# Where in SBUF the split weights of four SwiGLUs begin

## The chip, the cores and the metric

One core of one Trainium2 chip runs the whole program. The metric is the device time of one execution in microseconds, as the median of several. A smaller number is better. Input arrays lie in HBM in the layout that the kernel wants; the output is the full trunk's output for 512 tokens of 1024 channels.

## The reference

Two layers of a streaming encoder, each with a SwiGLU, a mixer and a second SwiGLU. Only what the change touches, the SwiGLUs, is shown in full; the mixer has two attentions, a pooling branch and a gated sum.

```python
D_MODEL, SEQ, DEPTH, D_FF = 1024, 512, 2, 2816

def swiglu(h, w_gate, w_up, w_down):
    return (jax.nn.silu(h @ w_gate) * (h @ w_up)) @ w_down

def reference(x, c, ...):
    c_act = jax.nn.silu(c)
    for l in range(DEPTH):
        mod = (c_act @ w_ada[l] + b_ada[l]).reshape(B, N_MOD, D_MODEL)
        h = modulate(rms_norm(x, norm_gain[l, 0]), mod[:, 0], mod[:, 1])
        x = x + 0.5 * mod[:, 2][:, None, :] * swiglu(h, ffn_w_gate[l, 0], ffn_w_up[l, 0], ffn_w_down[l, 0])
        h = modulate(rms_norm(x, norm_gain[l, 1]), mod[:, 3], mod[:, 4])
        x = x + mod[:, 5][:, None, :] * hybrid_mixer(h, w_in[l], ...)
        h = modulate(rms_norm(x, norm_gain[l, 2]), mod[:, 6], mod[:, 7])
        x = x + 0.5 * mod[:, 8][:, None, :] * swiglu(h, ffn_w_gate[l, 1], ffn_w_up[l, 1], ffn_w_down[l, 1])
    return x
```

All numbers are float32.

## The kernel before

**Numbers.** Every float32 operand of a large product is split into a high part `hi` (float32r) and a low part `lo` (the rest). A product then takes three matmuls, issued by `triple` (lines 119 to 121): hi times hi, lo times hi, hi times lo. A matmul loads 128x128 numbers as the stationary operand ("weights", engine row PEld) and streams 256 or 512 columns of the other operand past them (row PE). In the profile's names `acc<-b,whi`, the streamed operand stands first and the stationary one second.

**Weights.** A block of weights of 512 KB comes by DMA from the SP queue into a `raw` buffer; ScalarE copies it to float32r (`hi`), VectorE subtracts (`lo`). `wchunk` (line 250) does this for one block at a time, into a buffer of the pool's tag `whi` and one of `wlo`, of which there are three each. In the text below such a block is a *plain chunk*. The loads for the next SwiGLU or mixer, which are made early, go to `ptb` and `b` buffers instead (`spare`).

**A SwiGLU** (class `Ffn`, instances (layer, which) = (0,0), (0,1), (1,0), (1,1)) goes through the 22 blocks of 128 hidden channels in four parts of 6, 6, 4 and 6 (`PARTS`). Each part computes gate and up for its blocks and then adds its share of the down projection to x. A part's blocks are taken in three ways:

- as plain chunks, with all 512 tokens streamed at once (512 columns): some blocks of part 0, and the up half of its pairs;
- in pairs (`gate_up_pair`, line 609): two blocks are multiplied as a 2 by 2 block matrix with the tokens in two halves, in seven block products instead of eight. A pair takes 7 products of 4 x 3 matmuls, each of 256 columns. `pair_weights` (line 527) loads the two blocks, and makes sums and differences of them. Gate pairs (`which` 0) hold their weights in `ptb`, `v2` and `strip`; up pairs (`which` 1, in parts 1 to 3: 8 pairs in each SwiGLU) hold three of the four weight blocks in `whi` and `wlo`, which serve six of the seven products, and the fourth in `v2`;
- the down projection (`k_outer`, line 384) takes plain chunks of 256 x 512 weights, and streams 512 columns, in the very last half 256.

**Order.** The program is written out by Python; a tile framework puts the waits in. Each engine takes its instructions in the order written. DMA issues stand in the queue of the engine that issues them; the SP queue is strictly in order, so an issue that waits holds all that stand behind it. A buffer of a tag may be written again when its last reader is done. A small load takes part in the change: `forget` (line 954) loads 64 numbers a partition of `w_f` into the one buffer `wf`, once a layer, at the start of the mixer; and `send` in `attention` (line 1084) copies row sums into the one buffer `flat`, eight times a layer, from which a DMA of the POOL queue stores them.

**Places in SBUF.** The pool lays its buffers one behind the other. In the built program the `whi`, `wlo`, `b`, `xv` and `v2` buffers begin at multiples of 512 bytes, and `hhi` and `hlo` (the normed input, split) at multiples of 256. `raw`, `pta`, `ptb` and `strip` begin 32 bytes past a multiple of 64. Slices used by one matmul lie a multiple of 512 bytes further in, so that these remainders hold for every matmul operand named here.

Of the kernel before, what the change touches and what calls it, by code (L numbers as in the profile page):

```python
# [40 lines left out]
def encoder_kernel(tc, xT, c, w_ada, b_ada, gains, w_gate, w_up, w_down, w_qkv, w_f, w_ubg,  # L41
# [208 lines left out]
    def wchunk(src, shape, side=True, spare=None, lo_eng=None, home=None):  # L250
        if lo_eng is None:
            lo_share[1] += 1
            lo_eng = nc.gpsimd if lo_share[0] and lo_share[1] % lo_share[0] == 0 else nc.vector
        if quiet[0] > 0:
            quiet[0] -= 1
            if quiet[0] == 0:
                gate.clear()
        elif side and flow["on"] and mod_tag[0] == "v2":
            side_work()
        raw = st([P] + list(shape), F32, *(home or (("b", NB) if spare else ("raw", NRAW))))  # L260
        last["dma"] = nc.sync.dma_start(raw, src).ins
        if spare == "ptb":
            both = st([P, 2] + list(shape), F32R, "ptb", 2)
            hi, lo = both[:, 0], both[:, 1]
        elif spare == "b":
            hi = st([P] + list(shape), F32R, "b", NB)
            lo = st([P] + list(shape), F32R, "b", NB)
        else:
            hi = st([P] + list(shape), F32R, "whi", 3)
            lo = st([P] + list(shape), F32R, "wlo", 3)  # L270
        with behind("scalar"):
            nc.scalar.copy(hi, raw)  # L272
        with behind("vector"):
            last["lo"] = lo_eng.tensor_tensor(lo, raw, hi.bitcast(F32), op=ALU.subtract).ins  # L274
        return hi, lo
# [167 lines left out]
    PARTS = (6, 6, 4, 6)  # L443
    UP_FROM = 1
    SPIN = (4, 0, 7, 3)


    class Ffn:
# [78 lines left out]
        def pair_weights(self, n, which=0):  # L527

            shape = [P, 2, 4, P]
            d = []  # L530
            if which:
                d = [(st(shape, F32R, "whi", 3), st(shape, F32R, "wlo", 3)) for _ in range(3)]
                both = st(shape, F32R, "v2", 4)
                e = (both[:, 0], both[:, 1])
            else:
                for _ in range(2):
                    both = st([P, 2] + shape[1:], F32R, "ptb", 2)
                    d.append((both[:, 0], both[:, 1]))
                d.append((st(shape, F32R, "v2", 4), st(shape, F32R, "v2", 4)))
                e = (st([P, 4, P], F32R, "strip", 2), st([P, 4, P], F32R, "strip", 2))  # L540
            r = [st(shape, F32, *(("raw", NRAW) if which else ("b", NB))) for _ in range(2)]
            for i in range(2):
                last["dma"] = nc.sync.dma_start(r[i].rearrange("p a k c -> p (a k) c"),
                                                (w_gate, w_up)[which][self.l, self.s, n + i]).ins
            s3 = st([P, 4, P], F32, "ssum", 1)
            a11, a12, a21, a22 = r[0][:, 0], r[0][:, 1], r[1][:, 0], r[1][:, 1]
            g = nc.vector.tensor_tensor

            def sums():
                split_to(*d[0], r[0])  # L550
                g(s3, a11, a21, op=ALU.subtract)
                g(a21, a21, a22, op=ALU.add)

            def more():
                g(a11, a21, a11, op=ALU.subtract)
                g(a12, a12, a11, op=ALU.subtract)
                split_to(*d[2], r[0])

            steps = [sums, lambda: split_to(*d[1], r[1]), more, lambda: split_to(*e, s3)]
            w = lambda i, j: (d[i][0][:, j], d[i][1][:, j])  # L560
            tiles = {"a11": w(0, 0), "a12": w(0, 1), "s1": w(1, 0), "a22": w(1, 1), "s2": w(2, 0), "s4": w(2, 1), "s3": e}
            return tiles, steps
# [99 lines left out]
        def run(self, nxt):  # L662
            l, s, ms = self.l, self.s, self.ms
            mod_tag[0] = "v2"
            f0 = 0
            for part, nf in enumerate(PARTS):
                flow.update(on=True, behind="norm", **ADA_FFN(l, s, part))
                acts = []
                n = 0
                if part == 0 and self.norm is None:  # L670
                    acts = self.start()
                    acts += self.plain((3, 4, 5), None)
                    n = 6
                elif part == 0:
                    g0, u0, g1 = self.pre
                    pg, pu, pg1 = mmt(), mmt(), mmt()
                    for hs in range(2):
                        self.norm.back(hs, acc if hs else mmt)
                        cols = slice(hs * HALF, (hs + 1) * HALF)
                        if hs == 0:  # L680
                            later(FRONT1, lambda: self.norm.front(1, acc))
                            later(BACK1, lambda: self.norm.back(1, acc))
                        for k in range(KD):
                            self.unit(pg, g0, cols, (k,))
                            self.unit(pu, u0, cols, (k,))
                        self.unit(pg1, g1, cols)
                        if hs == 0:
                            u1 = self.gate_up(1, 1)
                    acts.append(self.act(0, pg, pu))
                    pu1 = mmt()  # L690
                    self.unit(pu1, u1)
                    acts.append(self.act(1, pg1, pu1))
                    acts += self.plain((2, 3), self.norm)
                    n = 4
                if part == 0 and n < nf:
                    self.ready, steps = self.next_pair(4, True)
                    for z in steps:
                        z()
                while n < nf:
                    acts += self.gate_up_pair(f0 + n, n + 2 < nf, part >= UP_FROM)  # L700
                    n += 2
                mod_need(l, 3 * ms + 2)
                last = part == len(PARTS) - 1
                for c0 in (0, T):
                    def src(c):
                        r0 = (f0 + 2 * c) * P
                        return w_down[l, s, r0:r0 + 2 * P, c0:c0 + T].rearrange("(k p) c -> p k c", p=P)

                    def ops(hi, lo, kt, j):
                        return (hi[:, j * P:(j + 1) * P], lo[:, j * P:(j + 1) * P],  # L710
                                acts[kt][:, 0, :], acts[kt][:, 1, :])

                    if last and c0 == 0 and nxt is not None:
                        nxt.prefetch("v2")
                        mod_tag[0] = "raw"
                    split = last and c0 > 0
                    hook, then = None, None
                    if split:
                        hook = nxt.prefetch_weights if nxt is not None else (lambda: None)
                    elif c0 > 0:  # L720
                        def then(n=f0 + nf):
                            self.ready, steps = self.next_pair(n, not last)
                            for i, z in enumerate(steps):
                                later(8 * i, z)
                    for j, hs, o in k_outer(src, nf // 2, ops, hook, acc if c0 == 0 else mmt, then):
                        d = c0 // P + j
                        residual_tail(d, hs, o, modc[:, l, 3 * ms + 2, d:d + 1], nxt if last else None)
                        if last and nxt is None:
                            cols = slice(0, T) if hs is None else slice(hs * HALF, (hs + 1) * HALF)
                            nc.sync.dma_start(out[:, d, cols], xd(d)[:, cols])  # L730
                f0 += nf
# [273 lines left out]
    def attention(qs, ks, vs, strip, ys, filler, budget, group):  # L1005
# [78 lines left out]
        def send(p):  # L1084
            rs = st([P, 2 * NT], F32, "rs", 1)
            nc.vector.reciprocal(rs, sums[p])
            tp = mmt()
            nc.tensor.transpose(tp[:2 * NT, :P], rs, ident)
            flat = st([2 * NT, P], F32, "flat", 1)
            nc.scalar.copy(flat, tp[:2 * NT, :P])  # L1090
            pe[0] += 0.5
            nc.gpsimd.dma_start(inv_dram[group, p], flat)
            later(LAG_R, lambda: spread(p), group)
# [119 lines left out]
    class Mixer:  # L1213
# [10 lines left out]
        def run(self, nxt):  # L1224
            l = self.l
            flow["on"] = False
            for b in range(4):
                nc.gpsimd.dma_start(x_dram[b], x_blocks[b].rearrange("p a t -> p (a t)"))
            g = qkgc[:, l, :]
# [163 lines left out]
```

## Time and profile before

| | |
|---|---|
| median of 3 runs | 2378.53 us (2377.65 to 2382.12) |
| the profiled execution | 2377.12 us |
| its span, first to last instruction | 2375.4 us |
| PE / PEld busy | 2356.8 us (99%) / 2092.4 us (88%) |
| DVE / ACT / POOL busy | 1781.4 (75%) / 1168.7 (49%) / 190.6 us (8%) |
| DMA engines | 41% busy on average, 137 GB/s |

The profiled execution is 1.7 us longer than its span, and 1.4 us shorter than the median. A matmul's row has its start, which is measured, and a length whose end is modelled; successive matmuls overlap, so that the pace is the distance from start to start and not the length. The four SwiGLUs lie at about 0 to 372, 814 to 1211, 1211 to 1548 and 1990 to 2375 us of the span, with a mixer between the first two and between the last two.

### The profile page before, as it was taken

To read this page: it belongs to the slowest core of one execution; us is meant where nothing else is said; L and a number is where in the kernel's file an instruction comes from. 1 tells how busy PE (TensorE), PEld (TensorE's weight loads), DVE (VectorE), ACT (ScalarE), POOL (GpSimd) and SP (SyncE) were. 2 spreads that over 40 slices of the span, in tenths; PEclk is the share of its full clock that TensorE was granted. 3 is DMA by queue.
4 is the path that set the end of the run, shared out by engine and by line. 5 is a ranking of instruction groups with operands and counts; after the bars stand their busy time and mean duration, and the time that the engine had idled before them with its cause. 6 is when DMAs were issued, how large, how long until landed. Compare 5 with 4: busy or idle time off the path is not lost. (4 is left out here: it accounts for less than half of the span.)

```text
span 2375.4 us, 36727 instructions
## 1 busy us (share of the span) xinstructions
PE 2356.8 (99%) x14172; PEld 2092.4 (88%) x14172; DVE 1781.4 (75%) x3213; ACT 1168.7 (49%) x2048; POOL 190.6 (8%) x309
## 2 busy tenths in 40 slices
PE   8999999999999999999999999999999999999999
PEld 6898998788888898999998999988888888989998
DVE  7888876787678477888678778776866774767784
ACT  5354455676532353544554444556765324544452
POOL 2000002122220000000100000120222101000000
PEclk9999999999999999999999999999999999999999
DMA  7634433333367425344325333423243763223232
GB/s 278 207 104 155 148 125 99 95 98 120 123 211 265 154 68 187 111 137 150 109 87 188 128 104 134 160 89 99 87 136 114 260 233 133 89 98 123 64 116 89
DMA packets 118484, 325.19 MB, mean 137 GB/s; under 512 B 12034, under 2 KB 14338, under 8 KB 118308
## 3 DMA queue, kind: packets, MB, share of 16 engines
q1 hardware_dynamic: 115106, 314.38, 39.5%
q0 software_dynamic: 3200, 8.46, 1.1%
q8 instruction: 111, 1.82, 0.3%
q14 instruction: 65, 0.53, 0.1%
q10 hardware_dynamic: 2, 0.00, 0.0%
HBM read 316.35 MB, written 6.44 MB: 136 GB/s over the span
## 5 line engine op out<-in xcount | busy, mean ns | idle before, releaser
L272 ACT CAST whi<-raw 128x1024 fp32r<-128x1024 f32 (+1 forms) x260 | 270.4, 1044 | 345.5 <-PE acc L120 196.2
L274 DVE TENSOR_TENSOR wlo<-raw,whi 128x1024 fp32r<-128x1024 f32 (+1 forms) x254 | 310.1, 1225 | 155.1 <-ACT whi L272 153.2
L120 PE MATMUL acc<-b,whi 128*128 128x512 f32 (+1 forms) x704 | 261.1, 371 | 2.0 <-DVE b L381 2.0
L119 PE MATMUL acc<-b,whi 128*128 128x512 f32 (+1 forms) x704 | 262.3, 373 | 0.0
L121 PE MATMUL acc<-b,wlo 128*128 128x512 f32 (+1 forms) x704 | 260.4, 370 | 1.2 <-DVE wlo L274 1.2
L121 PE MATMUL mm<-b,wlo 128*128 128x256 f32 (+1 forms) x768 | 244.8, 319 | 0.3 <-DVE wlo L274 0.3
L120 PE MATMUL mm<-b,whi 128*128 128x256 f32 (+1 forms) x768 | 244.5, 318 | 0.0
L119 PE MATMUL mm<-b,whi 128*128 128x256 f32 (+1 forms) x768 | 244.5, 318 | 0.0
L198 DVE CUSTOM_DVE_ANT_0 v<-v,b,badac 128x1024 f32<-128x1024 f32 x144 | 187.2, 1310 | 19.6 <-DMA v<-in_w_ada_dram 19.5
L120 PE MATMUL mm<-hlo,whi 128*128 128x256 f32 (+1 forms) x616 | 199.1, 323 | 0.0
L121 PE MATMUL mm<-hhi,wlo 128*128 128x256 f32 (+1 forms) x616 | 199.0, 323 | 0.0
L119 PE MATMUL mm<-hhi,whi 128*128 128x256 f32 (+1 forms) x616 | 198.7, 323 | 0.0
L120 PE MATMUL acc<-hlo,whi 128*128 128x512 f32 x480 | 188.1, 392 | 1.7 <-DVE hlo L788 1.6
L119 PE MATMUL acc<-hhi,whi 128*128 128x512 f32 x480 | 187.9, 396 | 1.1 <-ACT hhi L785 1.1
L121 PE MATMUL acc<-hhi,wlo 128*128 128x512 f32 x480 | 187.6, 391 | 0.0
L380 ACT CAST whi<-raw 128x1024 fp32r<-128x1024 f32 x96 | 100.8, 1050 | 136.0 <-PE mm L120 68.0
L121 PEld LDWEIGHTS mm<-b,wlo 128*128 128x128 f32 x768 | 146.3, 190 | 11.2 <-DVE wlo L274 1.2
L120 PEld LDWEIGHTS mm<-b,whi 128*128 128x128 f32 x768 | 146.3, 191 | 10.2
L119 PEld LDWEIGHTS mm<-b,whi 128*128 128x128 f32 x768 | 146.3, 191 | 10.1
L120 PEld LDWEIGHTS acc<-b,whi 128*128 128x128 f32 x704 | 132.7, 189 | 25.2 <-DVE b L381 3.8
L121 PEld LDWEIGHTS acc<-b,wlo 128*128 128x128 f32 x704 | 132.6, 188 | 24.2 <-DVE wlo L274 1.7
L119 PEld LDWEIGHTS acc<-b,whi 128*128 128x128 f32 x704 | 132.7, 189 | 21.6
(326 smaller groups left out, 6116.9 us busy)
## 6 DMA issues: line engine op xcount, KB each, us to landing
v<-in_w_ada_dram SPq DMA_DIRECT2D x144, 512.0 KB, 4.8
raw<-in_w_down_dram SPq DMA_DIRECT2D x88, 512.0 KB, 3.9
raw<-in_w_up_dram SPq DMA_DIRECT2D x82, 512.0 KB, 3.6
b<-in_w_gate_dram SPq DMA_DIRECT2D x76, 512.0 KB, 6.0
raw<-in_w_ubg_dram SPq DMA_DIRECT2D x56, 512.0 KB, 4.1
raw<-in_w_qkv_dram SPq DMA_DIRECT2D x42, 512.0 KB, 4.0
raw<-in_w_branch_dram SPq DMA_DIRECT2D x24, 512.0 KB, 3.6
raw<-in_w_out_dram SPq DMA_DIRECT2D x16, 512.0 KB, 3.7
```

The lines of the kernel that those rows point to most:

```text
L119: mm(o, lh, rh, start=start, stop=False, skip_group_check=onto)
L120: mm(o, lh, rl, start=False, stop=False, skip_group_check=onto)
L121: mm(o, ll, rh, start=False, stop=stop, skip_group_check=onto)
L198: dot = nc.vector.tensor_tensor_reduce(out=raw, in0=raw, in1=silc[0], scale=1.0, scalar=badac[:, l, j, d:d + 1], op0=ALU.mult, op1=ALU.add ...
L272: nc.scalar.copy(hi, raw)
L274: last["lo"] = lo_eng.tensor_tensor(lo, raw, hi.bitcast(F32), op=ALU.subtract).ins
L380: nc.scalar.copy(hi, src)
```

## The change

Three things are changed.

1. The `whi` and `wlo` buffers that `pair_weights` and `wchunk` use are made 16 numbers (64 bytes) longer, and the weights are put some numbers behind the buffer's start. In an up pair the distance is `SHIFT`: 8, 4, 12 and 2 numbers, which are 32, 16, 48 and 8 bytes, in SwiGLU (0,0), (0,1), (1,0) and (1,1). In a plain chunk of these SwiGLUs it is `PLAIN`: 0, 4, 2 and 1 numbers, or 0, 16, 8 and 4 bytes. In the mixers it is 0.
2. To make room, `flat` loses its own buffer and takes turns in that of `wf`.
3. By the longer buffers, `whi` and `wlo` now follow each other at 4160 bytes, so they begin at multiples of 64 bytes, no more always of 512; and all buffers behind them lie 384 bytes further on.

```diff
@@ wchunk
         else:
-            hi = st([P] + list(shape), F32R, "whi", 3)
-            lo = st([P] + list(shape), F32R, "wlo", 3)
+            n, z = int(np.prod(shape)), flow.get("z", 0)
+            names = "abc"[:len(shape)]
+            hi, lo = (st([P, D + 16], F32R, t, 3)[:, z:z + n]
+                      .rearrange(f"p ({' '.join(names)}) -> p {' '.join(names)}", **dict(zip(names, shape)))
+                      for t in ("whi", "wlo"))
@@
     SPIN = (4, 0, 7, 3)
+    PLAIN = {(0, 0): 0, (0, 1): 4, (1, 0): 2, (1, 1): 1}
+    SHIFT = {(0, 0): 8, (0, 1): 4, (1, 0): 12, (1, 1): 2}
@@ Ffn.pair_weights
             if which:
-                d = [(st(shape, F32R, "whi", 3), st(shape, F32R, "wlo", 3)) for _ in range(3)]
+                z = SHIFT[self.l, self.s]
+                d = [tuple(st([P, D + 16], F32R, t, 3)[:, z:z + D].rearrange("p (a k c) -> p a k c", a=2, k=4)
+                           for t in ("whi", "wlo")) for _ in range(3)]
@@ Ffn.run
             f0 = 0
+            flow["z"] = PLAIN[l, s]
@@ send
-            flat = st([2 * NT, P], F32, "flat", 1)
+            flat = st([2 * NT, P], F32, "wf", 1)
@@ Mixer.run
             flow["on"] = False
+            flow["z"] = 0
```

No engine gets another instruction, and PE, DVE and ACT keep theirs in the same order. One DMA issue moves in the SP queue: the load of `w_f` for the second layer, because its buffer is now also that of the first layer's `flat`. Before, it stands in the first layer's mixer, near the start; `raw` are weight blocks (w_qkv, w_down), and DMAHW marks a wait for an earlier DMA of the SP queue:

```order
L261 DMA raw_3628<-in_w_down_dram 128x2x512 [waits DMAHW6_49,DVE_49]
L261 DMA raw_4008<-in_w_qkv_dram 128x2x512 [waits DMAHW7_49,DVE_49]
L261 DMA raw_4086<-in_w_qkv_dram 128x2x512 [waits DMAHW3_49,DVE_49]
L956 DMA wf_16368<-in_w_f_dram 128x64 [waits DVE_49]
L261 DMA raw_4116<-in_w_qkv_dram 128x2x512 [waits DMAHW4_49,DVE_49]
```

With the change the same place in the SP queue reads:

```order
L261 DMA raw_3628<-in_w_down_dram 128x2x512 [waits DMAHW6_49,DVE_49]
L261 DMA raw_4008<-in_w_qkv_dram 128x2x512 [waits DMAHW7_49,DVE_49]
L261 DMA raw_4086<-in_w_qkv_dram 128x2x512 [waits DMAHW3_49,DVE_49]
L261 DMA raw_4116<-in_w_qkv_dram 128x2x512 [waits DMAHW4_49,DVE_49]
L261 DMA raw_4146<-in_w_qkv_dram 128x2x512 [waits DMAHW5_49,DVE_49]
```

The load is gone from there. It now stands at the end of the first layer's second attention. Before, the SP queue had there the last weight blocks of the attention's filler, then `w_pool` (`t`) and the silu of c (`b<-sil`), each for the work after the attention:

```order
L261 DMA raw_6948<-in_w_ubg_dram 128x1024 [waits DMAHW7_49,DMAHW2_49,DVE_49]
L261 DMA raw_6999<-in_w_ubg_dram 128x1024 [waits DMAHW0_49,DVE_49]
L261 DMA raw_7060<-in_w_branch_dram 128x2x512 [waits DMAHW2_49,DVE_49]
L1166 DMA t_1300_6850<-in_w_pool_dram 128x4x128 [waits DMAHW5_49,DVE_49]
L1285 DMA b_6848<-sil_dram 128x1024 [waits DMASW5_49,DMASW4_49,PE_49]
L261 DMA raw_7066<-in_w_ubg_dram 128x1024 [waits DMAHW3_49,DVE_49]
```

With the change:

```order
L261 DMA raw_6948<-in_w_ubg_dram 128x1024 [waits DMAHW6_49,DMAHW1_49,DVE_49]
L261 DMA raw_6999<-in_w_ubg_dram 128x1024 [waits DMAHW7_49,DVE_49]
L261 DMA raw_7060<-in_w_branch_dram 128x2x512 [waits DMAHW1_49,DVE_49]
L964 DMA wf_16368<-in_w_f_dram 128x64 [waits DMASW4_49,DMASW5_49,DMASW3_49,DMASW6_49,DMASW2_49,DMASW7_49,DMASW1_49,DMAHW4_49,DMASW0_49,Activation_49]
L1174 DMA t_1300_6850<-in_w_pool_dram 128x4x128 [waits DVE_49]
L1294 DMA b_6848<-sil_dram 128x1024 [waits DMASW5_49,DMASW4_49,PE_49]
L261 DMA raw_7066<-in_w_ubg_dram 128x1024 [waits DMAHW2_49,DVE_49]
```

The `w_f` load waits there for all eight stores of `flat` (DMASW are DMAs of the POOL queue), and the loads of `w_pool` and of the silu stand behind it.

## The prediction

> **What bounds the kernel now.** I read the first part of the page first, then the list of who waited for whom.
>
> ```profile
> PE 2356.8 (99%) x14172; PEld 2092.4 (88%) x14172; DVE 1781.4 (75%) x3213; ACT 1168.7 (49%) x2048; POOL 190.6 (8%) x309
> PE mm L145 <- ACT b L133: 3.7, 1, 3.7
> PE acc L120 <- DVE b L381: 2.0, 3, 0.8
> ```
>
> The time is that of the matmuls following each other: of 2375.4 us PE is busy for 99%, its longest wait in all is 3.7 us at the start, the next 2.0 us. So an edit counts by what it does to the pace of the matmuls, and hardly by anything else. To see the pace, I read the order of time on PE at three places: an up pair's product (256 columns, weights in `whi`), a gate pair's (256 columns, weights in `ptb`), and a plain chunk's (512 columns, `whi`).
>
> ```profile
> 958.00 0.28 PE L119 MATMUL mm<-hhi,whi 128*128 128x256 f32 x1
> ...
> 959.92 0.28 PE L120 MATMUL mm<-hlo,whi 128*128 128x256 f32 x1
> 967.71 0.28 PE L119 MATMUL acc<-hhi,ptb 128*128 128x256 f32 x1
> ...
> 969.83 0.28 PE L119 MATMUL acc<-hhi,ptb 128*128 128x256 f32 x1
> 2047.69 0.39 PE L120 MATMUL mm<-hlo,whi 128*128 128x512 f32 x1
> ...
> 2049.96 0.39 PE L121 MATMUL mm<-hhi,wlo 128*128 128x512 f32 x1
> ```
>
> There are 16, 18 and 10 steps between the two rows of each place. From start to start a matmul takes 1.92/16 = 120.0 ns with `whi`, 2.12/18 = 117.8 ns with `ptb`, and 2.27/10 = 227 ns at 512 columns. The same work, 256 columns against 128x128 weights, goes 2 ns faster in the gate pairs. The view of the instructions by tile, between 930 and 1180 us, shows how (min/median/max, in ns):
>
> ```profile
> L120 PE MATMUL mm<-hlo,whi x96: 283/283/283, 957.8 to 1160.8; 128*128 128x256 f32 x96
> L120 PEld LDWEIGHTS mm<-hlo,whi x96: 187/192/192, 957.6 to 1160.7; 128*128 128x128 f32 x96
> L120 PE MATMUL acc<-hlo,ptb x64: 277/281/285, 947.8 to 1145.1; 128*128 128x256 f32 x64
> L120 PEld LDWEIGHTS acc<-hlo,ptb x64: 187/188/191, 947.7 to 1145.0; 128*128 128x128 f32 x64
> ```
>
> With `whi` all 96 are alike: the stream keeps a **beat**. With `ptb` they vary from 277 to 285. The length is the pace plus 163 ns at both (283 - 120, 281 - 118) and 162 at 512 columns (389 - 227), so a difference of lengths is a difference of pace. What differs between the two is the place: `whi` begins at multiples of 64 bytes as `hhi` and `hlo` do, and `ptb` 32 bytes past one. That the place is the cause is inferred; the pairs differ in tokens and banks too. At 512 columns the sides are turned: the mixer's first products stream `ptb` past weights of `hhi`, again 32 bytes apart, between 370 and 388 us:
>
> ```profile
> L120 PE MATMUL acc<-ptb,hhi x16: 393/396/398, 372.5 to 386.8; 128*128 128x512 f32 x16
> ```
>
> At 512 columns off the beat is slower, 396 for 389; at 256 it is faster, 281 for 283.
>
> **The change, part by part.** I use lengths as pace, and count in one SwiGLU, (0,1), by the groups of its window, 866 to 1211 us:
>
> ```profile
> L120 PE MATMUL acc<-b,whi 128*128 128x512 f32 x88 | 34.4, 391 | 0.0
> L120 PE MATMUL mm<-b,whi 128*128 128x512 f32 x64 | 24.9, 389 | 0.0
> L120 PE MATMUL mm<-hlo,whi 128*128 128x512 f32 x56 | 21.8, 390 | 0.0
> L120 PE MATMUL mm<-b,whi 128*128 128x256 f32 x120 | 34.0, 283 | 0.0
> L120 PE MATMUL mm<-hlo,whi 128*128 128x256 f32 x96 | 27.2, 283 | 0.0
> ```
>
> Three lines issue the same count, so that a SwiGLU has 3 x (88 + 64 + 56) = 624 matmuls of 512 columns on plain chunks. Of the 120 + 96 of 256 columns, 96 + 96 are the up pairs' (8 pairs x 6 products x 4): 3 x 192 = 576. The other 24 belong to the down projection's last half, and are left out: at 2 ns they make 0.3 us a SwiGLU at most.
>
> *Up pairs, 4 x 576 = 2304 matmuls.* The only rows with weights 32 bytes off are those of `ptb` (and of `strip`, alike): a mean of 281.
>
> ```profile
> L119 PE MATMUL acc<-b,ptb 128*128 128x256 f32 x280 | 78.3, 280 | 0.0
> L120 PE MATMUL acc<-b,ptb 128*128 128x256 f32 x280 | 78.8, 282 | 0.0
> ```
>
> (0,0), 32 bytes: 576 x -2 ns = -1.2 us. No row has 16, 48 or 8 bytes. The ends are every matmul as the fastest with `ptb`, 277, or the slowest, 285: -6 or +2 ns, so -3.5 to +1.2 us for each SwiGLU, -13.8 to +4.6 us for all four. 16 and 48 bytes lie midway between a row that keeps the beat (0, and 64, which is 0 again) and one that doesn't (32): I take half, -0.6 us each. 8 bytes is nearest to 0: I take nothing. Sum -2.4 us.
>
> *Plain chunks.* The ends at 512 columns are 388, the fastest with `whi` in that view, and 396:
>
> ```profile
> L119 PE MATMUL acc<-b,whi x64: 388/389/395, 1007.7 to 1178.2; 128*128 128x512 f32 x64
> ```
>
> -1 or +7 ns, times 624, is -0.6 to +4.4 us for each of three SwiGLUs, -1.9 to +13.1 us in all. (0,1), 16 bytes: half again, +2.2 us. (1,0) and (1,1), 8 and 4 bytes: nearest to 0, nothing. (0,0) is not moved.
>
> *Weights not shifted* (mixers and the plain chunks of (0,0)): their buffers may begin at odd multiples of 64 bytes, which no row shows. I take nothing, as `ptb` buffers, 32 off, and `whi`, 0 off, are the only two kinds seen; if it counts, it is the case of +7 ns at over 2000 matmuls of 512 columns, some +15 us.
>
> *Copies and subtractions into the shifted buffers.* With `ptb`, 32 bytes off, they take what they take with `whi`:
>
> ```profile
> L380 ACT CAST whi<-raw 128x1024 fp32r<-128x1024 f32 x96 | 100.8, 1050 | 136.0 <-PE mm L120 68.0 <-DVE raw L552 20.0 <-PE mm L121 14.7
> L381 DVE TENSOR_TENSOR wlo<-raw,whi 128x1024 fp32r<-128x1024 f32 x96 | 117.2, 1220 | 23.3 <-ACT whi L380 23.2
> L381 DVE TENSOR_TENSOR ptb<-b,ptb 128x1024 fp32r<-128x1024 f32 x70 | 85.6, 1222 | 32.0 <-ACT ptb L380 31.6
> ```
>
> Nothing, and ACT waits 136 us there, mostly for PE, so a few ns more are hidden; if DVE lost a tenth on each, 122 ns x some 300 would be 37 us of an engine that idles 25% of the span.
>
> *The load of `w_f` in the SP queue.* Once, it waits for the last store of `flat` and holds two loads behind it:
>
> ```profile
> 647.21 0.51 POOL L1092 DMA_DIRECT2D inv_dram_c<-flat  x1 [8.65 <-ACT flat L1090]
> DMA to landing us min/median/max: 1.5/2.0/3.1
> 648.08 0.38 SPq L261 DMA_DIRECT2D raw<-in_w_branch_dram  x1
> 648.55 0.42 SPq L1166 DMA_DIRECT2D t<-in_w_pool_dram  x1
> 660.53 2.07 SPq L261 DMA_DIRECT2D raw<-in_w_ubg_dram  x2
> 652.79 0.62 ACT L380 CAST pta<-t 128x512 fp32r<-128x512 f32 x1 [2.02 <-DMA t<-in_w_pool_dram]
> 656.19 0.62 ACT L380 CAST b<-b 128x512 fp32r<-128x512 f32 x1 [2.78 <-DVE b L1105]
> ```
>
> The store lands at 647.21 + 2.0 = 649.2 (at most 650.3), so `w_pool` goes out 1.1 to 2.2 us after its 648.55, behind an issue of 0.4. ACT's copy of it starts that much later than 652.79; ACT's next work starts at 656.19 after 2.78 us of idle time, which covers it. The third load behind goes at 660.53 anyhow. I take 0; uncovered it is +2.2 us once.
>
> Sum: -2.4 + 2.2 = -0.2 us, on an execution of 2377.1 us; the median of the runs is 1.4 us above that, 2378.5. **Forecast: 2378.0 us**, no change that can be measured: 0.2%, 4.8 us, is about what a measurement of this kernel can tell.
>
> **Rivals.**
>
> (a) *The place doesn't matter.* Then `ptb` and `whi` differ by what they multiply, and the time is 2378.5. Speaking for it: no two rows differ in place alone. Against: products with `whi` are all 283 whether `hhi` or sums stand against them. The Trainium skill ("TensorE: Matmul & The Clock Gate", Step-by-step: what each phase is for) says that weights come through a read port of their own, so that loading them takes no bandwidth from the running matmul; by that rule the shift is worth nothing, and the weight loads of 192 against 188 ns above are the row that it doesn't explain.
>
> (b) *Slower: short distances break the beat at 512 columns.* If 8 bytes and 4 do what 32 does, plain chunks take 396 for 389. With 16 and 8 bytes off the beat it is +4.4 x 2 = 8.7 us, against 2304 x -2 ns = -4.6: +4.1, 2382.6. With 4 too it is +13.1 - 4.6 = +8.5, 2387.0. It decides from the second SwiGLU that loses the beat. For it: the beat's exactness (283/283/283) looks like a fit that a small step could spoil. Against: a beat that returns after every stop looks like one that takes small steps.
>
> (c) *Faster: the up pairs reach a shorter beat.* The single matmuls of 277 show that 114 ns is possible; a place where all do that gives up to -13.8, a mean of 3 to 6 ns -7 to -13.8, so 2364.7 to 2371.6, if the plain chunks stay. For it: 16, 48 and 8 bytes are new places, and one beat is known to exist. Against: `ptb`'s and `strip`'s never settle there. The Trainium skill ("TensorE: Matmul & The Clock Gate", Back-to-back issue gap) gives 2.5 ns over the columns' own time between matmuls, an estimate of 109 ns at 256 columns against 120 here, which would be -25 us over the up pairs; no run here shows it.
>
> **How the numbers follow.** Forecast 0.40 (2376 to 2381), (a) 0.10, (b) 0.25 (a small part of it the unshifted weights, above 2387), (c) 0.25. Faster by over 0.2% is (c) and the edge of the forecast: 0.27. Slower is (b): 0.25. Within: 0.48. The range reaches over most of (b) and (c): 2366 to 2387.
>
> **What would show it.** In the view by tile, for each SwiGLU apart: up pairs at 281 and spread in (0,0), at 283/283/283 in (1,1); plain chunks of 389 in (1,0) and (1,1). A median of 396 there is (b); 280 or less without spread is (c); all unchanged, (0,0) too, is (a). PE's waits should stay under 10 us, and the copy of `w_pool` start near 654 without a wait on PE behind it; a wait there, or slower copies on DVE, would be what I left out.

## The result and the profile after

The change makes the kernel slower: 2397.3 us (median of 4 runs, 2392.99 to 2397.8) against 2379.69 us for the kernel before on the same chip (4 runs, 2377.65 to 2382.12), a ratio of 1.0064, 95% interval 1.0052 to 1.0077. That is 17.6 us by the medians; the recorded ratio weighs the runs otherwise, and its interval is 12 to 18 us. The profiled execution took 2397.63 us, its span is 2395.9 us, 20.5 us longer than the one before, at a granted clock of 0.999.

The first part of the page and the list of who waited for whom:

```profile
PE 2375.8 (99%) x14172; PEld 2091.8 (87%) x14172; DVE 1782.4 (74%) x3213; ACT 1165.3 (49%) x2048; POOL 191.1 (8%) x309
```

```profile
PE mm L145 <- ACT b L133: 4.2, 1, 4.2
PE acc L121 <- DVE wlo L277: 2.6, 1, 2.6
PE acc L120 <- DVE b L384: 1.5, 3, 1.0
```

The other engines do what they did, and PE's longest waits are nearly as small as before. PE alone is 19.0 us busier, with the same 14172 matmuls: what has changed is, but for one stop that is shown below, the pace of the matmuls. The view by tile between 930 and 1180 us, in SwiGLU (0,1), has the same three kinds as the prediction's rows (min/median/max in ns):

```profile
L120 PE MATMUL mm<-hlo,whi x96: 277/281/285, 966.3 to 1171.3; 128*128 128x256 f32 x96
L119 PE MATMUL acc<-b,whi x64: 389/395/403, 930.3 to 1179.9; 128*128 128x512 f32 x64
L120 PEld LDWEIGHTS mm<-hlo,whi x96: 187/188/189, 966.1 to 1171.2; 128*128 128x128 f32 x96
```

The up pairs, 283/283/283 before, have lost their beat and look as the products with `ptb` did, 2 ns shorter. The plain chunks have gone from a median of 389 to one of 395, which is 6 ns longer. So far it could be the 16 bytes of this SwiGLU. But the same is seen where no weights are shifted. In the mixer, between 600 and 800 us, the first row is of before and the second of after:

```profile
L119 PE MATMUL acc<-hhi,whi x190: 387/389/478, 600.0 to 799.9; 128*128 128x512 f32 x190
```

```profile
L119 PE MATMUL acc<-hhi,whi x184: 387/392/508, 602.7 to 798.2; 128*128 128x512 f32 x184
```

And in SwiGLU (0,0), whose plain chunks lie 0 bytes into their buffers, by groups of its window, 0 to 372 us (busy us, mean ns), before and after:

```profile
L121 PE MATMUL mm<-hhi,wlo 128*128 128x512 f32 x64 | 24.9, 389 | 0.0
```

```profile
L121 PE MATMUL mm<-hhi,wlo 128*128 128x512 f32 x64 | 25.2, 393 | 0.0
```

I added up, over all matmuls of a kind, the distances from each start to the next one, in the trace of after and in that of before, and took the difference:

| matmuls | after less before, us |
|---|---|
| 512 columns, weights not shifted: (0,0), and both mixers | +4.8, and +4.9 |
| 512 columns in the windows of (0,1), shifted by 16, (1,0), by 8, (1,1), by 4 bytes | +4.2, +3.1, +3.9 |
| up pairs: (0,0) 32, (0,1) 16, (1,0) 48, (1,1) 8 bytes | -0.7, -0.4, +0.4, -0.6 |
| other 256 columns with `whi`, `wlo` | -1.5 |
| gate pairs, whose weights the change doesn't touch | +1.7 |
| all else | +0.6 |

Together that is +20.4 of the 20.5 us. These distances contain PE's stops, and the 4.8 us of (0,0) are pace for 2.1 only. The rest comes from one place where PE stops three times between 189 and 193 us; behind it seven matmuls go at 427 ns from start to start, at a granted clock of 0.50 (last row: the stretch, busy time, matmuls, clock, DMA). The trace of before has stops there too, but no such stretch:

```profile
192.52 0.60 PE L120 MATMUL acc<-b,whi 128*128 128x512 f32 x1 [0.96 <-DVE b L384]
192.92 0.63 PE L121 MATMUL acc<-b,wlo 128*128 128x512 f32 x1
...
195.48 0.63 PE L121 MATMUL acc<-b,wlo 128*128 128x512 f32 x1
193.00:195.00 2.00, 2.00 (x6) 0.50 1.00 399
```

With stops left out, the 512 columns lose some 17.5 us, and 7.0 of these, 2.1 in (0,0) and 4.9 in the mixers, are in matmuls whose weights are not shifted at all. What happened to them is that their buffers, 4160 bytes apart, begin at 0, 64 and 128 (`whi`) and 192, 0 and 64 (`wlo`) bytes past multiples of 256.

### The profile page after: what moved, and what is told of

Read it like the earlier page. It is cut to its first block, busy times and chain, and to the rows that moved or that the text cites. A ratio compares the mean times of both kernels' runs of the same rounds, so it can differ in the third digit from the quotient of the medians.

```text
span 2395.9 us, 36728 instructions
## 1 busy us (share of the span) xinstructions
PE 2375.8 (99%) x14172; PEld 2091.8 (87%) x14172; DVE 1782.4 (74%) x3213; ACT 1165.3 (49%) x2048; POOL 191.1 (8%) x309
```

## The experiments

Two theories stood after the comparison. By the first, **the place** counts: what the start of the weights leaves over, against the streamed operand's, sets the pace, and the longer buffers spoil it by themselves. By the rival, it is the **shifts**, and the unshifted matmuls are slower for a reason of their own: the load of `w_f`, the move of all buffers behind by 384 bytes, or disturbance from the neighbours. "Pace" below is the mean distance from start to start of successive matmuls of a kind, waits left out, from the profiled execution; before it is 119.9 ns in the up pairs and 227.0 to 227.3 ns at 512 columns. To make room for longer buffers, some kernels have 16 `b` buffers for 17. All of them have `flat` in the buffer of `wf`, but for e2.

**e1: the longer buffers alone.** The change with every shift at 0:

```
-    PLAIN = {(0, 0): 0, (0, 1): 4, (1, 0): 2, (1, 1): 1}
-    SHIFT = {(0, 0): 8, (0, 1): 4, (1, 0): 12, (1, 1): 2}
+    PLAIN = {(0, 0): 0, (0, 1): 0, (1, 0): 0, (1, 1): 0}
+    SHIFT = {(0, 0): 0, (0, 1): 0, (1, 0): 0, (1, 1): 0}
```

> All buffers as in the change (whi and wlo 64 bytes longer, flat in wf's buffer), but every shift 0. Theory 'starts': the loss comes from buffers that begin at odd multiples of 64 bytes, so it stays: 512-column matmuls on whi/wlo at a mean of 393 to 394 ns everywhere, +16 to +20 us, within 3 us of the change. Theory 'shifts': the distance inside the buffer costs in the plain chunks of three SwiGLUs (10.6 us of the 20.9 between the two traces); without it +9 to +11 us, and the plain chunks of (0,1), (1,0) and (1,1) near the 389 of before or no worse than those of (0,0).

Measured: 2390.03 us, ratio 1.0039 (1.0025 to 1.0053). Of the 17.6 us that the change costs, 10.8 (by the ratio's interval 6 to 13) are there with no weights shifted within their buffers. In the trace the matmuls of 512 columns cost 16.6 us more than before (some 14 with stops left out), at a pace of 230.3 to 230.9 ns in all four SwiGLUs, and the up pairs 5.4 us less, at 117.6 to 117.8 ns. Matmuls of (1,1) between 2048 and 2070 us, before and in e1:

```profile
L119 PE MATMUL mm<-hhi,whi x33: 389/389/389, 2048.1 to 2069.9; 128*128 128x512 f32 x33
```

```profile
L119 PE MATMUL mm<-hhi,whi x26: 389/392/404, 2052.4 to 2069.7; 128*128 128x512 f32 x26
```

So the pace is lost by the starts alone, as the first theory has it. The time isn't within 3 us of the change's, as it should have been by that theory; the rest has to come from the shifts.

**e2: the control for one buffer less.** The kernel before with 16 `b` buffers:

```
-    NB, NRAW = 17, 2
+    NB, NRAW = 16, 2
```

> The kernel before with 16 instead of 17 buffers of tag b (4 KB freed), everything behind them 4096 bytes lower, no shift, whi and wlo as before. Both theories: the beat stays (389 at 512 columns, 283 at 256); the time within 4 us of before, unless PE waits for a b buffer. It is the control of the next two.

Measured: 2378.98 us, 0.9993 (0.9983 to 1.0002): no difference, so kernels with 16 may be compared with the one before.

**e3: the shifts alone.** The change's shifts, in buffers 512 bytes longer, so that all of them begin at multiples of 512 bytes as before:

```
-    NB, NRAW = 17, 2
+    NB, NRAW = 16, 2
-            hi, lo = (st([P, D + 16], F32R, t, 3)[:, z:z + n]
+            hi, lo = (st([P, D + 128], F32R, t, 3)[:, z:z + n]
-                d = [tuple(st([P, D + 16], F32R, t, 3)[:, z:z + D]
+                d = [tuple(st([P, D + 128], F32R, t, 3)[:, z:z + D]
```

> As e2, with the change's shifts, but buffers of whi and wlo 512 bytes longer instead of 64, so that each begins at a multiple of 512; flat in wf's buffer. Theory 'starts': no loss, within 2 us of e2, plain chunks at 389 to 390. Theory 'shifts': plain chunks of (0,1), (1,0), (1,1) at 394 to 395, +8 to +11 us over e2; mixers and (0,0) plain at 389; up pairs at 281, -1 us or so.

Measured: 2380.82 us, 1.0004 (0.9993 to 1.0014). With clean starts the shifts cost nothing that can be measured on the whole, but they aren't without effect: in the trace the 512 columns lose 6.1 us and the up pairs gain 4.9. This is the kernel in which the prediction's distances can be read one by one, and they say the opposite of it at 512 columns: 227.2 ns at 0, 230.0 at 16, 230.7 at 8 and 231.9 at 4 bytes. The smallest step costs most. In SwiGLU (1,1), by groups (8 bytes for the up pair in the first row, 4 for the plain chunk in the second):

```profile
L120 PE MATMUL mm<-hlo,whi 128*128 128x256 f32 x96 | 26.7, 278 | 0.0
L120 PE MATMUL mm<-hlo,whi 128*128 128x512 f32 x56 | 22.1, 394 | 0.0
```

The up pairs' pace is 118.3 ns at 32, 16 and 48 bytes alike, and 115.7 at 8 bytes.

**e4: the up pairs' shifts alone.** As e3, with the plain chunks back at 0:

```
-    PLAIN = {(0, 0): 0, (0, 1): 4, (1, 0): 2, (1, 1): 1}
+    PLAIN = {(0, 0): 0, (0, 1): 0, (1, 0): 0, (1, 1): 0}
```

> As e3 with only the up pairs shifted (32, 16, 48, 8 bytes), plain chunks 0. Both theories: plain chunks keep 389; the up pairs go from 283 to a mean near 281 (they did in the change: 281.3, 281.5, 282.2, 280.6), so 2304 x -1.5 ns = -3.5 us against e2 at most; if an up pair at the new place is slower from start to start, up to +1 us.

Measured: 2374.76 us, 0.9978 (0.9968 to 0.9988), faster than the kernel before. The plain chunks have their beat again, in (1,1) by the view by tile between 2048 and 2070 us:

```profile
L119 PE MATMUL mm<-hhi,whi x33: 389/389/389, 2047.7 to 2069.4; 128*128 128x512 f32 x33
```

The 6.1 us between e3 and e4 are the whole price of the plain chunks' shifts. With e1 this makes a square: neither 2379, the shifts alone 2380.8, the longer buffers alone 2390.0, both 2397.3. The two don't just add up: on top of the longer buffers the shifts cost 7.3 us, on clean starts 1.6. By the traces of e1 and of the change, 4.3 of these are lost at 512 columns, and 4.1 by the up pairs, which gained 5.4 us in e1 and 1.3 in the change.

**e5: the load of `w_f` alone.** The kernel before with one edit:

```
-            flat = st([2 * NT, P], F32, "flat", 1)
+            flat = st([2 * NT, P], F32, "wf", 1)
```

> The kernel before with only flat moved into wf's buffer, so that the w_f load of the second layer waits in the SP queue. As predicted: 0, at most +2.2 us. Rival: the held loads cost, +2 us or more and a new wait on PE near 650 us.

Measured: 2379.65 us, 0.9999 (0.9989 to 1.0010). The queue's new order costs nothing that these runs can tell (-2.6 to +2.4 us).

**e6: the buffers behind moved, `whi` and `wlo` as before.** As e5, with 384 unused bytes behind `wlo`:

```
+    st([P, 96], F32, "pad", 1)
     badac = cp.tile([P, L, 9, KD], F32, name="badac")
```

> As e5 with whi and wlo as before, and all buffers behind them 384 bytes further on, as in the change. Theory 'starts': remainders of 512 count, not of 64, so the gate pairs (ptb from 288 to 160, v2 from 0 to 384 past a multiple of 512) change pace as in the change and in e1: 118.6 to 119.0 ns, +1.5 us in all; plain chunks stay at 227 ns from start to start. Rival: remainders of 64 alone count; nothing changes, 0.

Measured: 2382.21 us, 1.0013 (1.0003 to 1.0022). A small part of the loss, some 3 us (0.7 to 5.2), comes from here. The gate pairs go from 118.6 to 119.2 ns, 2.1 us in all, much as in e1 and with the change. The move puts `ptb` and `strip` from 32 to 160 bytes past multiples of 256, and `v2` from 0 to 128. In the trace the gate pairs' products with `ptb` get slower, from 118.2 to 119.7 ns, and those with `v2` faster, from 119.7 to 118.5. By multiples of 64, nothing would have changed.

**e9 and e10: steps of 128 and of 256 bytes.** As e1, with buffers 128 and 256 bytes longer (`pair_weights` likewise, not shown), and 16 `b` buffers:

```
-            hi, lo = (st([P, D + 16], F32R, t, 3)[:, z:z + n]
+            hi, lo = (st([P, D + 32], F32R, t, 3)[:, z:z + n]
```

```
-            hi, lo = (st([P, D + 16], F32R, t, 3)[:, z:z + n]
+            hi, lo = (st([P, D + 64], F32R, t, 3)[:, z:z + n]
```

> As e2, with whi and wlo 128 bytes longer, no shift: they begin at 0, 128, 256 and 384 past multiples of 512. If the pattern repeats every 128 bytes, plain chunks keep 227 ns from start to start; if every 256 or 512, they go to about 230, +10 us.

> As e2, with whi and wlo 256 bytes longer, no shift: they begin at 0 and 256 past multiples of 512. hhi begins 256 past a multiple of 512 and keeps the beat with whi at 0, so I expect 227 and 120 ns, no change; if 512 is the step that counts, about 229 to 230 ns, +6 to +10 us.

One run each: 2394.34 and 2378.35 us, against 2379.96 for one run of the kernel before. Matmuls of (1,1) between 2048 and 2070 us, first at steps of 128, then at steps of 256 bytes:

```profile
L119 PE MATMUL mm<-hhi,whi x19: 389/393/404, 2057.4 to 2069.9; 128*128 128x512 f32 x19
```

```profile
L119 PE MATMUL mm<-hhi,whi x33: 389/389/389, 2047.9 to 2069.7; 128*128 128x512 f32 x33
```

With buffers at 0 and 128 past multiples of 256 the beat is lost (230.1 to 230.5 ns), with all of them at 0 past 256 it is kept, though half of them are then at odd multiples of 256. What counts is the remainder by 256 bytes.

**e8: all six buffers 64 bytes off, alike.** The kernel before with 16 `b` buffers, `flat` in `wf`, 64 unused bytes ahead of `whi` and 448 behind `wlo`, so that nothing else moves:

```
+        if b == 0:
+            st([P, 16], F32, "pad", 1)
...
+    st([P, 112], F32, "pad2", 1)
```

> As e2, with all six buffers of whi and wlo 64 bytes past a multiple of 512, alike, and what lies behind on the remainders of before. Theory 'distance to the stream': the beat needs weights and streamed operand on the same remainder, so the plain chunks go off it, 230 to 231 ns from start to start for 227, +9 to +14 us. Theory 'unlike each other': what breaks the beat in e1 is that the buffers begin at six different remainders; alike, 227 ns and 120 ns stay, 0.

One run: 2392.2 us against 2379.44 (median of 27). With one remainder for all of them there is a beat again, another one at each width. The view by tile, up pairs between 966 and 1172 us and plain chunks between 2048 and 2070:

```profile
L120 PE MATMUL mm<-hlo,whi x95: 276/276/281, 965.9 to 1168.6; 128*128 128x256 f32 x95
```

```profile
L119 PE MATMUL mm<-hhi,whi x18: 393/398/398, 2057.4 to 2069.3; 128*128 128x512 f32 x18
```

And the order of time on PE at an up pair's start:

```profile
1160.62 0.28 PE L119 MATMUL mm<-hhi,whi 128*128 128x256 f32 x1
...
1161.98 0.28 PE L119 MATMUL mm<-hhi,whi 128*128 128x256 f32 x1
```

There are 12 steps in 1.36 us, 113.3 ns each, against 120.0. At 512 columns it is 233.3 ns throughout, against 227. The same place is the best one seen at 256 columns and the worst at 512: the up pairs gain 12.6 us and the 512 columns lose 27.3.

**e7 and e11: a better place for the up pairs alone.** As e4, all up pairs 8 bytes off, and all 64 bytes off:

```
-    SHIFT = {(0, 0): 8, (0, 1): 4, (1, 0): 12, (1, 1): 2}
+    SHIFT = {(0, 0): 2, (0, 1): 2, (1, 0): 2, (1, 1): 2}
```

```
-    SHIFT = {(0, 0): 2, (0, 1): 2, (1, 0): 2, (1, 1): 2}
+    SHIFT = {(0, 0): 16, (0, 1): 16, (1, 0): 16, (1, 1): 16}
```

> As e4 (whi and wlo on multiples of 512, plain chunks unshifted) with all four SwiGLUs' up pairs 8 bytes off. If the 115.8 ns of (1,1) in e4 belongs to the 8 bytes, all four run at 115.8 for 120.0: 2304 x -4.1 = -9.5 us, of which the stalls (1.8 us in (1,1) of e4) give back up to 7 us: -2.5 to -9.5 us against before. If it belongs to (1,1), the others stay at 118 to 120 and the time is within 2 us of e4.

> Buffers whi and wlo begin at multiples of 512 bytes, plain chunks are not shifted, and the up pairs' weights lie 64 bytes off in all four SwiGLUs. Theory (the place within 256 bytes sets the pace, and only the place of the weights that a matmul takes against its streamed operand): the up pairs go from 120.0 to 113.4 ns from start to start, as where all six buffers began 64 bytes off; 2304 x -6.6 ns = -15 us, of which waits for ACT and DVE take back 2 to 6 us, since 8 bytes off (115.8 ns) already showed 2 us of them in the last two SwiGLUs. Plain chunks stay at 227 ns. Time 2366 to 2371 us. Rival (the supply is the limit): PE is faster while it runs, but waits for the next pair's weights by all that it gains past 8 bytes: 2373 to 2375 us, as with 8 bytes. Rival (what counted there was that the buffers themselves begin 64 bytes off, so that the copies write there too and follow each other otherwise): the pace is not 113 ns, the time 2374 us or above.

Measured: 2374.31 us, 0.9980 (0.9971 to 0.9988), and 2370.93 us, 0.9965 (0.9951 to 0.9978). In (0,1), 8 bytes and 64 bytes:

```profile
L120 PE MATMUL mm<-hlo,whi x84: 277/278/284, 975.3 to 1159.0; 128*128 128x256 f32 x84
```

```profile
L120 PE MATMUL mm<-hlo,whi x84: 276/276/286, 973.5 to 1156.4; 128*128 128x256 f32 x84
```

Both beats hold (115.8 and 113.4 ns), and the plain chunks keep 389. For e11 the matmuls alone are worth 2304 x 6.5 ns = 15 us; the up pairs' sum falls by 9.3. The rest is in gaps between the up pairs' matmuls, 6.0 us by the distances of over 135 ns. The larger part of them is in the list of waits: PE waits there until ScalarE has copied a finished product out of its bank (`kept`, line 591), a wait that the list of before doesn't have (8 bytes, then 64 bytes):

```profile
PE mm L119 <- ACT t L591: 2.2, 5, 0.6
```

```profile
PE mm L119 <- ACT t L591: 3.4, 7, 0.8
```

**e12 and e14: the gate pairs too, and `v2`.** e12 is e11 with 32 unused bytes ahead of `raw`, so that `ptb` and `strip` go from 32 to 64 past multiples of 256; e14 is e12 with `v2` 64 off as well:

```
             for d in range(KD):
+            if l == 0 and self.s == 0:
+                st([P, 8], F32, "pad", 1)
```

```
+            if l == 0 and self.s == 0:
+                st([P, 16], F32, "padv", 1)
...
-                st([P, 8], F32, "pad", 1)
+                st([P, 56], F32, "pad", 1)
```

> As the kernel with the up pairs 64 bytes off, and with 32 bytes of unused room ahead of raw, pta, ptb and strip, which then begin 64 instead of 32 bytes past a multiple of 256. Theory (place): the gate pairs' products with ptb and strip go from 118.5 to 113.4 ns as well; 35 pairs with 60 such matmuls are 2100 x -5 ns = -10 us, less waits for ACT and DVE of 2 to 6 us. Products of 512 columns that stream ptb stay near 396 ns long. Time 2358 to 2366 us. Rival (the supply is the limit): the gate pairs are followed closely by ACT and DVE, the gain goes into PE's waits, and the time is that of the kernel without the room within 2 us. Rival (ptb's spread comes from what it multiplies and not from its place): gate pairs stay at 118 ns or above, the time too.

> As the kernel with up pairs and gate pairs 64 bytes off, and v2 as well (64 bytes of room ahead of it, and 224 ahead of raw in place of 32, so that raw, ptb and strip stay 64 past a multiple of 256). v2 holds the weights of one of the seven products of each pair, and two plain chunks in each SwiGLU's end are streamed against it. Theory (place): some 1200 matmuls with v2 as weights go from 119.7 to 113.4 ns, -6.3 x 1200 = -7.6 us, less waits for ACT and DVE; where v2 is streamed past whi (64 + 32 matmuls of 512 columns) +3 to 6 ns each, +0.6 us. Time 2361 to 2367 us. Rival (the supply is the limit): PE waits by what it gains, and the time is 2367 to 2370 us.

Measured: 2368.47 us, 0.9945 (0.9932 to 0.9957), and 2368.48 us, 0.9955 (0.9941 to 0.9968). These are the fastest kernels of the study, though their intervals overlap with that of e11. Neither of the theories had it right; the time of e14 lies where its rival put it, but PE's waits shrank, so that this is luck. In e12 some of the gate pairs' products took the shorter beat and others didn't. The pace of those with `ptb` fell to 116.0 ns, not to 113.4, that of whole gate pairs to 117.3, 3.9 us in all for the 10 that I had expected. The two groups, products with `ptb` in e12 between 930 and 1180 us, and in e14 the up pairs of the same stretch:

```profile
L120 PE MATMUL acc<-hlo,ptb x64: 276/276/281, 944.9 to 1140.8; 128*128 128x256 f32 x64
```

```profile
L120 PE MATMUL mm<-hlo,whi x84: 281/281/281, 973.1 to 1155.2; 128*128 128x256 f32 x84
```

Before, the first was 277/281/285. With `v2` at 64 as well, every product of an up pair has its weights at one remainder (in the seventh, `pta` is streamed, which lies at 64 too, in e12 as in e14), and still the pairs settle at 281, a mean pace of 117.2 ns, where they ran at 276 with `v2` at 0. Waiting isn't the reason, since the waits for that copy, 3.4 us in e11, are smaller in e14:

```profile
PE mm L119 <- ACT t L591: 1.4, 3, 0.5
```

The order of time shows that at this distance there are two beats. In an up pair of e14 PE stops once, after the third product. The matmuls on both sides have the same distance:

```profile
305.52 0.28 PE L119 MATMUL mm<-hhi,whi 128*128 128x256 f32 x1
...
309.64 0.28 PE L121 MATMUL mm<-b,wlo 128*128 128x256 f32 x1
309.99 0.38 PE L119 MATMUL mm<-b,whi 128*128 128x256 f32 x1
...
310.46 0.28 PE L119 MATMUL mm<-b,whi 128*128 128x256 f32 x1
...
311.59 0.28 PE L120 MATMUL mm<-b,whi 128*128 128x256 f32 x1
```

Ahead of the stop it is 35 steps in 4.12 us, 117.7 ns each, and behind it 10 in 1.13 us, 113 ns. Of the 32 up pairs of e14, 27 keep to 281 in their products with `whi` and `wlo`, 3 to 276, and 2 go from one to the other, each right after such a stop; other stops change nothing. A gate pair of e12 changes without a stop, across the product with `v2` at 0:

```profile
967.62 0.28 PE L121 MATMUL acc<-b,ptb 128*128 128x256 f32 x1
...
968.30 0.28 PE L121 MATMUL acc<-b,ptb 128*128 128x256 f32 x1
...
969.85 0.28 PE L119 MATMUL acc<-b,ptb 128*128 128x256 f32 x1
...
971.14 0.28 PE L121 MATMUL acc<-b,ptb 128*128 128x256 f32 x1
```

Ahead of the `v2` product it is 6 steps in 0.68 us, 113.3 ns, and behind it 11 in 1.29 us, 117.3 ns. So a matmul's pace hangs not on its own two operands alone: the distance allows more than one beat, and what ran before decides between them. By what rule stays open.

**e13: both operands moved together.** The kernel before with 16 `b` buffers, `flat` in `wf`, and 64 unused bytes ahead of `hhi`. Everything that the products named here read is 64 bytes further on, so that all distances are as before:

```
+    cp.tile([P, 16], F32, name="pad")
     hhi = cp.tile([P, KD, T], F32R, name="hhi")
```

> The kernel before with 64 bytes of unused room ahead of hhi, so that hhi, hlo, b, whi, wlo and v2 all begin 64 bytes past a multiple of 256, and ptb, raw and strip 96: every distance between weights and streamed operand is what it was. Theory (the distance between the two operands counts): all paces as before, 120.0 ns at 256 columns and 227 ns at 512, and the time that of the kernel before within 0.2%, 2376 to 2383 us. Rival (the weights' own place counts, whatever the streamed operand's): the paces of the kernel where only whi and wlo lay 64 bytes off, 233 ns at 512 columns and 113.4 ns in the up pairs, and 2390 to 2395 us.

Measured: 2379.09 us, 0.9993 (0.9984 to 1.0002), with the paces of the kernel before, in (0,1):

```profile
L120 PE MATMUL mm<-hlo,whi x84: 283/283/284, 977.1 to 1161.1; 128*128 128x256 f32 x84
```

`whi` and `wlo` lie where they lay in e8, and none of e8's effect is there. So it is the **distance** between the weights and the streamed operand that sets the pace, not the weights' own place, with the reserve from e12 and e14 that one distance can have two beats.

## Why the prediction was wrong

The forecast was 2378.0 us, the range 2366 to 2387; measured 2397.3. What bounds the kernel, the pace of the matmuls and not any wait, was right, and so was the proxy that a difference of lengths is one of pace. Point by point:

- **The step that failed: weights not shifted, taken at nothing.** The prediction saw that these buffers may begin at odd multiples of 64 bytes and took 0, since only two places had rows, and reckoned 64 bytes as "0 again". No row showed that the remainder by 64 is the one that counts. It is the remainder by 256 (e9, e10), and the longer buffers alone cost 10.8 us (e1), with 230.3 to 230.9 ns at 512 columns for 227. The prediction had the price in hand, "+7 ns at over 2000 matmuls", some 15 us, but gave it a small part of one rival, and the range ended below it.
- **Plain chunks, +2.2 us.** At clean starts they cost 6.1 us (e3 less e4). 16 bytes was sized about right, +2.8 ns where +3.5 was taken. 8 and 4 bytes, taken at nothing as nearest to 0, are +3.5 and +4.7 ns: nearness to 0 is worth nothing. That is the mechanism of rival (b), at half to two thirds of its price.
- **Up pairs, -2.4 us.** At clean starts -4.9 (e3). 32 bytes were right, 118.3 ns for 118. 16 and 48 bytes are worth the same as 32, not half, and 8 bytes, taken at nothing, the most. In the change itself only -1.3 us is left of it, since its buffers' starts are mixed.
- **Copies and subtractions, nothing:** DVE 1782.4 us for 1781.4, ACT 1165.3 for 1168.7. Right.
- **The load of `w_f`, nothing.** Right (e5). In the order of time after, the load of `w_pool` goes out at 653.83, ACT waits 4.00 us for it where it waited 2.02, and idles 0.36 us before its next work where it idled 2.78:

```profile
653.83 0.43 SPq L1174 DMA_DIRECT2D t<-in_w_pool_dram  x1
659.25 0.62 ACT L383 CAST pta<-t 128x512 fp32r<-128x512 f32 x1 [4.00 <-DMA t<-in_w_pool_dram]
660.23 0.62 ACT L383 CAST b<-b 128x512 fp32r<-128x512 f32 x1 [0.36 <-DVE b L1113]
```

  The cover of 2.78 us was nearly used up, and no wait on PE came of it. In the whole kernel's time it isn't seen.
- **Not in the sum at all: the buffers behind,** moved by 384 bytes. The text of the change said so; the prediction gave it no term. It is some 3 us (e6).
- **Rival (a), the place doesn't matter,** is refuted by e1, e7, e8 and e11, which differ from the kernel before in places, and beside that only in the edits that e2 and e5 show to cost nothing. The Trainium skill ("TensorE: Matmul & The Clock Gate", Step-by-step: what each phase is for) holds that a weight load takes no read bandwidth from the running matmul. These runs don't show bandwidth itself, but e8 and e13 have the same weight loads at the same addresses, and at 512 columns they differ by 6 ns a matmul: where the streamed operand lies relative to the weights is not free of cost in a stream that loads weights for every matmul.
- **Rival (c), a shorter beat,** exists, at 64 bytes off (113.4 ns) and 8 bytes off (115.8), but not at the places that the change chose for three of the four SwiGLUs. The shortest steady pace at 256 columns in any run is 113.3 ns (e8), so that a pace of 109 ns, as rival (c) ends with, was not reached.

The time of the change is then the sum of e1's 10.8 us, of which e6's 3 are a part, and of the shifts on top of it, 17.6 - 10.8 = 6.8 us (7.3 by the two medians, whose runs of the kernel before are different ones), where the prediction had -0.2 us for the shifts.

## What to carry to other kernels

A buffer made longer moves every buffer behind it: list the start of each matmul operand after such a change, and its distance from the operand that it meets, modulo a power of two that is large enough (here 256 bytes, not 64), before any time is put on the edit. Where a kernel is bound by the pace of its matmuls, try places for each width apart: here 64 bytes off gained 5% at 256 columns and lost 3% at 512, and the 2371 us of e11 came from giving each its own. A place that no row shows has an unknown cost and belongs in the range with both its signs, even if two neighbouring places look alike.

## What the runs showed of the hardware

The steadiest beats are 113.4 and 119.9 ns at 256 columns, 227.0 and 233.3 ns at 512; the other means lie between these. By distance of the weights from the streamed operand, modulo 256 bytes, for float32r matmuls of 128x128 weights that load new weights each time (the mean of the up pairs, and of plain chunks; one profile each, granted clock 0.999 or 1.0):

| distance, bytes | 256 columns, ns | 512 columns, ns | from |
|---|---|---|---|
| 0 | 119.9 | 227.0 to 227.3 | before, e13 |
| 4 | | 231.9 | e3 |
| 8 | 115.8 | 230.7 | e7, e3 |
| 16 | 118.3 | 230.0 | e3 |
| 32 and 48 | 118.3 | | e3 |
| 64 | 113.4 | 233.3 | e8, e11 |
| 64, `v2` too | 117.0 to 117.7 | | e14 |
| 0 and 128 in turn | 119.3 | 230.1 to 230.5 | e9 |
| 0, 64, 128 and 192 in turn | 117.6 to 117.8 | 230.3 to 230.9 | e1 |

The order is not that of the distance, and of the four distances seen at both widths the fastest at one is the slowest at the other. Why the distance counts, and why most up pairs run at 113.4 ns with `v2` at 0 and at 117.7 with `v2` at 64 (e12 against e14), no run here tells.

Behind a stop of PE some matmuls of 512 columns go at 427 ns, as those at 193 us in the trace of after at a granted clock of 0.50. Ten of the sixteen traces have such a stretch, of five to twelve matmuls. At 200 ns more than the usual pace each, it makes 1 to 2.4 us, and two executions can differ by that without any difference in place.
